# Later block loads and transposes, and a state copied on ScalarE, in a hybrid RWKV-7 and pooling layer

## Chip, cores, metric

One core of one Trainium2 chip runs the whole layer. The metric is the device time of one execution in microseconds (us); the median of several executions counts.

## What is computed

One layer on 1024 latent and 256 context tokens, model width 2048: RMS norm with modulation, one input projection whose columns feed an RWKV-7 time-mixing branch (16 heads of 64, two directions) and a pooling branch, gates on both, one output projection, a residual and a last norm. What the change touches is the scan of the time-mixing branch:

```python
def _rwkv_step(S, inp):
    r, w, k, v, a, b = inp
    sa = jnp.einsum('dbhvk,dbhk->dbhv', S, a)
    S = S * w[..., None, :] + sa[..., :, None] * b[..., None, :] + v[..., :, None] * k[..., None, :]
    y = jnp.einsum('dbhvk,dbhk->dbhv', S, r)
    return S, y
```

The state starts at zero, runs over the context tokens and then over the latent ones, forwards and backwards. The y of both directions are added, normalised per head, given a bonus, and multiplied by a gate.

## The kernel before

The scan is done in chunks of 64 tokens (20 chunks, 4 of them context). Four groups Q of four heads follow one another, so there are 80 steps: step k is one chunk of one Q, in both directions. Within a chunk the recurrence is a triangular system. Its matrices (the scores) are made by matmuls 20 steps ahead (`scores`, L758), copied by ScalarE and masked by GpSimd (`masked`, L771 and L772), and written to DRAM (sNM, L773). For 8 steps at a time VectorE inverts the diagonal 32x32 blocks of these matrices: `inverse` (L778) loads them as TT by four DMAs on SyncE's queue (L783), and then does 30 pairs of a multiply (L789) and an add (L791). `assemble` completes the inverses to 64x64 tiles T by two groups of small matmuls (L826, L837) through bank B0.

`run_step` (L1036) is one step:

- `phase_x` (L893): product of NA (scores and keys, from DRAM) and SUV. SUV holds, side by side on the partitions, the values from DRAM (`step_loads`, L856) and the state scaled to this step. VectorE copies the result to Xs (L896).
- the outputs of the step before (`outputs`, L935 and L937; L937 reads the state that was there before that step), then `step_loads`, `bk_load` and `score_loads` issue loads for later steps on SyncE.
- `phase_t` (L903): product with T; VectorE copies the result U into SUV (L904, L905).
- y is gathered (L957 on ScalarE, L959 on VectorE), and the scores of step k + 20 are made.
- `phase_s` (L915): the update of the state from BKt and SUV. VectorE adds the old state (St, L918) and multiplies by the decay PCt straight into the state's place in the next step's SUV, in two halves of 64 partitions (L922). GpSimd multiplies the same sum once more into the tile S (L923), which the next outputs and the next sum read.
- `turned` (L881, L882) transposes the keys of the next step on TensorE through bank B0 and ScalarE copies them to BKt; `masked` follows.
- `pump` fills TensorE with units of the gate, pooling and output columns of the input projection (dense units: twelve matmuls of 512 columns, L154 to L156, counted at UNIT = 2.65 us), 1.55 of them per step, or 2 where no scores are left to make.

What else VectorE does runs as threads, generators that `slot` and `invert` advance while a model of the time (`at`) has room: weight splits, gates, pooling, inversion, and `finish`, which normalises y (L972 to L985), loads bonus and gate (L992), transposes y through bank B0 (L1001), and combines them (L1008, L1010). In it `yield 0` ends the present slot, and `yield from later()` waits until one more dense unit has been issued, except where `rush` forces a thread through: when a new Q begins, `gathered` (L943) settles what is left of `finish`.

The order on TensorE, VectorE and ScalarE is the one in which the code issues (a manual schedule); that of SyncE and GpSimd is set by the framework's scheduler from readiness and code order. Each engine takes its queue in order. SyncE's DMAs share 8 semaphores in turn, so that a ninth waits for the first to land.

`begin(i)` (L1030) creates the inversion of batch i and issues its TT loads. In the step with k % 8 = 4 it runs at the end, after the scores' masks; the inversion's arithmetic starts in the step with k % 8 = 6, right behind Xs (`invert`, L1018).

Of the kernel before, what the change touches and what calls it, by code (L numbers as in the profile page):

```python
# [11 lines left out]
ALU = mybir.AluOpType  # L12
# [47 lines left out]
def hybrid_layer_kernel(ctx: ExitStack, tc: tile.TileContext, I, out, dbg=None):  # L60
    nc = tc.nc
    mm = nc.tensor.matmul
    V, S, G = nc.vector, nc.scalar, nc.gpsimd
# [9 lines left out]
    def nm(s):  # L73
        cnt[0] += 1
        return f"{s}_{cnt[0]}"

    def bank(tag, bufs=1):
        return psum.tile([128, 512], F32, tag=tag, bufs=bufs, name=nm("ps"))
# [108 lines left out]
    with ExitStack() as p0:  # L187
# [89 lines left out]
        for k in range(2):  # L277
            u = hc_pool.tile([128, NALL + 4], F32, tag="k", bufs=2, name=nm("ue"))
# [63 lines left out]
    for k in range(2):  # L342
        s, u = p1.tile([128, NALL], F32, tag="A", name=nm("s")), early[k]
# [213 lines left out]
    with ExitStack() as p2s:  # L557
# [7 lines left out]
        hss = [slice(64 * h, 64 * h + 64) for h in range(2)]  # L565
# [17 lines left out]
        def later():  # L583
            due = unit_no[0] + 1
            while unit_no[0] < due and not rush[0]:
                yield 0
# [255 lines left out]
        nas, suv, mrs, rts, bkts, ins = {}, {}, {}, {}, {}, {}  # L842
# [43 lines left out]
        def phase_x(k):  # L886
            NA, SUV = nas.pop(k), suv[k]
            if steps[k][1] + steps[k][2] == 0:
                st["S"] = st.pop("S0")
            XU = st["XU"] = bank("XU")  # L890
            for u in range(4):
                for h in range(2):
                    mm(XU[hss[h], 64 * u:64 * u + 64], NA[:, h, u // 2, u % 2, :], SUV[:, h, u // 2, u % 2, :],  # L893
                       start=True, stop=True)
            Xs = st["Xs"] = p2.tile([128, 4, C], F32, tag="Xs", name=nm("Xs"))
            V.tensor_copy(Xs.rearrange("q u v -> q (u v)"), XU[:, 0:256])  # L896
# [10 lines left out]
        def phase_s(k):  # L907
            Q, g, s = steps[k]
            c = CCH * g + s
            SUV, S0, DY = suv[k], st["S"], bank(("DY", "B1")[k % 2])  # L910
            if c < NCH - 1:
                BKt = bkts.pop(k)
                for u in range(4):
                    for h in range(2):
                        mm(DY[hss[h], 64 * u:64 * u + 64], BKt[:, u // 2, u % 2, h, :], SUV[:, h, u // 2, u % 2, :],  # L915
                           start=True, stop=True)
                tmp = p2.tile([128, 4, C], F32, tag="St", name=nm("St"))
                V.tensor_tensor(tmp.rearrange("q u v -> q (u v)"), DY[:, 0:256], S0.rearrange("q u v -> q (u v)"), ALU.add)  # L918
                Sn = p2.tile([128, 4, C], F32, tag="S", bufs=2, name=nm("S"))
                pc = PCt[:, Q, c].rearrange("q p d -> q (p d)").unsqueeze(2).broadcast_to([128, 4, C])  # L920
                for h in range(2):
                    V.tensor_tensor(suv[k + 1][hss[h], h].rearrange("q p d v -> q (p d) v"), tmp[hss[h]], pc[hss[h]], ALU.mult)  # L922
                G.tensor_tensor(Sn, tmp, pc, ALU.mult)  # L923
                st["S"] = Sn
            if g:
                st["late"] = k, S0, DY
            else:
                suv.pop(k)
# [37 lines left out]
        def finish(Q, m, y):  # L966
            runs = (C * (6 - 2 * m), C * (8 + 2 * m))
            js = slice(2 * Q, 2 * Q + 2)
            mean = p2.tile([128, 8], F32, tag="mean", bufs=2, name=nm("mean"))
            rs = p2.tile([128, 8], F32, tag="rs", bufs=2, name=nm("rs"))  # L970
            yf = y.rearrange("q p r c v -> q (p r c) v")
            V.tensor_reduce(mean, yf, mybir.AxisListType.X, ALU.add)  # L972
            V.tensor_scalar(mean, mean, 1.0 / C, None, op0=ALU.mult)
            yield 0.7
            V.tensor_tensor(yf, yf, mean.unsqueeze(2).broadcast_to([128, 8, C]), ALU.subtract)
            sq = p2.tile([128, 8, C], F32, tag="sqy", bufs=2, name=nm("sqy"))
            S.activation(sq, yf, AF.Square)
            yield 0.7
            yield from later()
            V.tensor_reduce(rs, sq, mybir.AxisListType.X, ALU.add)  # L980
            S.activation(rs, rs, AF.Sqrt, bias=eps_ln, scale=1.0 / C)
            yield 0.6
            yield from later()
            V.reciprocal(rs, rs)
            V.tensor_tensor(yf, yf, rs.unsqueeze(2).broadcast_to([128, 8, C]), ALU.mult)  # L985
            while gates_done[0] < 2 * Q + 2:
                unit()
            parts = []
            for src in (sBV, sG):
                t = p2.tile([128, 2, 2, 128], F32, tag="bvs", bufs=2 * BVS, name=nm("bvs"))  # L990
                for r in range(2):
                    dma(t[:, :, r], src[js, :, runs[r]:runs[r] + 128].rearrange("j q t -> q j t"))  # L992
                parts.append(t)
            yield 0.8
            yield 0
            while not dense[0] and not rush[0]:
                yield 0
            ps = bank("B0")
            for i in range(8):
                for h in range(2):  # L1000
                    mm(ps[hss[h], 64 * i:64 * i + 64], yf[hss[h], i, :], ident[hss[h], hss[h]], start=True, stop=True)  # L1001
            mx = p2.tile([128, 2, 2, 128], F32, tag="mxn", bufs=2, name=nm("mx"))
            for p in range(2):
                j = 2 * Q + p
                S.activation(mx[:, p].rearrange("q r t -> q (r t)"), ps[:, 256 * p:256 * p + 256], AF.Identity,
                             bias=lbs[:, j:j + 1], scale=lgs[:, j:j + 1])
            yield from later()
            V.tensor_tensor(mx, mx, parts[0], ALU.add)  # L1008
            yield 0.7
            V.tensor_tensor(mx, mx, parts[1], ALU.mult)  # L1010
            for r in range(2):
                idma(sM[js, :, runs[r]:runs[r] + 128].rearrange("j q t -> q j t"), mx[:, :, r])
            yield 0.7
# [16 lines left out]
        def begin(i):  # L1030
            if i < NST // 8:
                invs[i], invn[i] = inverse(i), 0
                next(invs[i])


        def run_step(k):  # L1036
            r = k % 8
            last = k == NST - 1
            phase_x(k)
            pe(0.7, st.get("suv", 0.0))  # L1040
            xs = dve(0.41, at["pe"])
            if r in (0, 5) and k // 4 + 1 < len(batches):
                asm["now"] = assemble(k // 4 + 1)
                next(asm["now"])
            late = st.pop("late", None)
            if late:
                outputs(*late)
                pe(1.7)
            else:
                unit()  # L1050
                owed[0] -= 1
            bk_load(k + 2)
            if not last:
                step_loads(k + 1)
            if k + LEAD + 2 < NST:
                score_loads(k + LEAD + 2)
            dense[0] = False
            invert(k, max(at["pe"], xs) + 0.5)
            slot(max(at["pe"], xs) + 0.4)
            phase_t(k)  # L1060
            pe(0.7, xs)
            us = dve(0.84, at["pe"])
            if late:
                gathered(*late)
                dve(0.56)
            if k + LEAD < NST:
                scores(k + LEAD)
                pe(1.7)
            elif unit_no[0] < NU:
                unit()  # L1070
                owed[0] -= 1
            if r in (2, 7) and "now" in asm:
                run(asm.pop("now"))
                pe(0.6)
            invert(k, max(at["pe"], us) + 0.5)
            slot(max(at["pe"], us) + 0.4)
            dense[0] = True
            phase_s(k)
            pe(0.7, us)
            st["suv"] = dve(1.48, at["pe"])  # L1080
            if not last:
                turned(k + 1)
                pe(0.6)
            if k + LEAD < NST:
                masked(k + LEAD)
            if r == 4:
                i = k // 8 + 1
                if i in invs:
                    run(invs.pop(i))
                begin(i + 1)  # L1090
            n = FILLS[k + LEAD >= NST]
            left = at["pe"] + UNIT * int(owed[0] + n) + 0.7
            slot(left - 1.2)
            invert(k, left)
            pump(n)
            if r in (1, 6) and "now" in asm:
                next(asm["now"])
                pe(0.6)
# [224 lines left out]
```

## Time and profile before

| what | us |
|---|---|
| median of 3 runs | 2368.15 |
| lowest and highest run | 2356.09, 2370.49 |
| the profiled execution | 2357.3 |
| its span, first to last instruction | 2355.5 |
| the scan's stretch in it | 1085 to 1955 |

The profile is of one execution. An engine's idle time counts only where it delays the end; a row's last part, in brackets or behind an arrow, is the idle time of the engine before that work and what ended it. PE is TensorE, DVE is VectorE, ACT is ScalarE, POOL is GpSimd, SPq is SyncE's queue of DMAs.

### The profile page before, as it was taken

How to read it: one execution, taken by the hardware profiler on the slowest of the kernel's cores; microseconds unless marked ns; L12 is line 12 of the kernel's file. 1: busy time of each engine (PE TensorE's matmuls, PEld its weight loads, DVE VectorE, ACT ScalarE, POOL GpSimd, SP SyncE). 2: the span in 40 equal slices, each digit the busy share in tenths (PEclk: the TensorE clock that was granted, in tenths of full speed). 3: DMA queues.
4: the chain of work that ended last, by engine and by line, in shares of the span. 5: the costliest groups of instructions: out<-in, count | busy, mean ns of one | idle time of the engine just before them, and what ended most of it. 6: DMA issues, size and time to landing. Idle time of an engine off the chain costs nothing. (4 is left out here: it accounts for less than half of the span.)

```text
span 2355.5 us, 49746 instructions
## 1 busy us (share of the span) xinstructions
PE 2155.2 (91%) x19854; PEld 1304.9 (55%) x19854; DVE 1474.1 (63%) x2544; ACT 849.3 (36%) x1447; POOL 514.0 (22%) x702
## 2 busy tenths in 40 slices
PE   2999999999999999989988989889799998999997
PEld 1445444454444444445655566556555664888886
DVE  7644756475476477456769767787586674445546
ACT  5344534344344344212223323323332223333424
POOL 3000000011000000244655555545443211000000
PEclk9999999999999999999999999999999999999999
DMA  8765555455343344796887788877877643645546
GB/s 307 232 211 171 141 146 149 140 150 154 100 127 96 104 127 112 221 299 193 249 238 226 212 237 243 258 220 231 232 232 198 187 136 104 219 130 170 192 129 206
DMA packets 494999, 437.19 MB, mean 186 GB/s; under 512 B 274328, under 2 KB 366520, under 8 KB 494512
## 3 DMA queue, kind: packets, MB, share of 16 engines
q1 hardware_dynamic: 473712, 366.88, 54.3%
q0 software_dynamic: 21056, 67.13, 8.4%
q8 instruction: 157, 2.57, 0.5%
q14 instruction: 74, 0.61, 0.1%
HBM read 316.68 MB, written 115.88 MB: 184 GB/s over the span
## 5 line engine op out<-in xcount | busy, mean ns | idle before, releaser
L154 PE MATMUL ps<-hhi,whi 128*128 128x512 f16 x1600 | 612.0, 383 | 1.6 <-DVE sg L686 0.8
L156 PE MATMUL ps<-hhi,wlo 128*128 128x512 f16 x1600 | 609.8, 381 | 0.6 <-DVE wlo L633 0.6
L155 PE MATMUL ps<-hlo,whi 128*128 128x512 f16 x1600 | 610.1, 382 | 0.0
L156 PEld LDWEIGHTS <-wlo 128*128 128x128 f16 x1888 | 185.5, 98 | 196.5 <-issue 17.5
L154 PEld LDWEIGHTS <-whi 128*128 128x128 f16 x1888 | 185.3, 98 | 192.4 <-issue 30.3
L155 PEld LDWEIGHTS <-whi 128*128 128x128 f16 x1888 | 185.8, 99 | 178.5 <-issue 21.8
L1181 PE MATMUL ps<-wolo,mhi 128*128 128x512 f32 x512 | 199.8, 390 | 2.7 <-DVE wolo L1177 2.6
L1181 PE MATMUL ps<-wohi,mlo 128*128 128x512 f32 x512 | 199.0, 389 | 0.0
L1181 PE MATMUL ps<-wohi,mhi 128*128 128x512 f32 x512 | 198.5, 390 | 0.0
L772 POOL TENSOR_TENSOR NM<-NM,mask 128x512 f32<-128x512 f32 (+1 forms) x140 | 177.8, 1288 | 54.9 <-ACT NM L771 51.0
L1177 DVE TENSOR_TENSOR wolo<-wo,wohi 128x512 fp32r<-128x512 f32 x144 | 98.2, 689 | 144.9 <-ACT wohi L1176 144.6
L147 DVE SCALAR_TENSOR_TENSOR wlo<-wraw,whi 128x512 f16<-128x512 f32 x104 | 70.6, 686 | 175.3 <-ACT whi L146 173.7
L1176 ACT CAST wohi<-wo 128x512 fp32r<-128x512 f32 x144 | 89.3, 621 | 174.6 <-PE ps L1181 156.3
L882 ACT COPY BKt<-ps 128x512 f32<-128x512 f32 x76 | 44.4, 584 | 283.3 <-PE ps L881 283.3
L896 DVE COPY Xs<-ps 128x256 f32<-128x256 f32 x80 | 33.8, 423 | 152.4 <-PE ps L893 152.1
L789 DVE TENSOR_TENSOR tm<-TT 128x30 f32<-128x30 f32 (+5 forms) x300 | 112.4, 375 | 14.0 <-DMA TT<-sNM 6.7
L923 POOL TENSOR_TENSOR S<-St,PCt 128x256 f32<-128x256 f32 x76 | 60.2, 792 | 264.4 <-DVE St L918 263.8
L791 DVE TENSOR_TENSOR TT<-TT,tm 128x30 f32<-128x30 f32 (+5 forms) x300 | 109.7, 366 | 10.3
L1181 PEld LDWEIGHTS ps<-wolo,mhi 128*128 128x128 f32 x512 | 96.1, 188 | 24.6 <-DVE wolo L1177 4.9
L1181 PEld LDWEIGHTS ps<-wohi,mhi 128*128 128x128 f32 x512 | 95.9, 188 | 21.0 <-ACT wohi L1176 1.0
L1181 PEld LDWEIGHTS ps<-wohi,mlo 128*128 128x128 f32 x512 | 96.1, 188 | 19.8
L758 PE MATMUL ps<-AR,BK 64*128 64x128 f32 (+1 forms) x1280 | 94.8, 289 | 8.2 <-issue 2.7
(232 smaller groups left out, 3523.7 us busy)
## 6 DMA issues: line engine op xcount, KB each, us to landing
wraw<-in_w_in SPq DMA_DIRECT2D x200, 256.0 KB, 3.8
BK<-sBK SPq DMA_DIRECT2D x156, 256.0 KB, 4.1
wo<-in_w_out SPq DMA_DIRECT2D x144, 256.0 KB, 2.9
sNM<-NM POOLq DMA_DIRECT2D x64, 512.0 KB, 5.4
wa<-in_w_ada SPq DMA_DIRECT2D x112, 256.0 KB, 3.3
wg<-in_w_ada SPq DMA_DIRECT2D x64, 256.0 KB, 3.0
AR<-sAR SPq DMA_DIRECT2D x64, 256.0 KB, 5.0
MR<-sNM SPq DMA_DIRECT2D x64, 256.0 KB, 3.3
```

The lines of the kernel that those rows point to most:

```text
L147: V.scalar_tensor_tensor(wlo, raw, WS, whi, op0=ALU.mult, op1=ALU.subtract)
L154: mm(ps[:, :n], w[0][:, k, :], hi[kt][:, o:o + n], start=(kt == 0), stop=False)
L155: mm(ps[:, :n], w[0][:, k, :], lo[kt][:, o:o + n], start=False, stop=False)
L156: mm(ps[:, :n], w[1][:, k, :], hi[kt][:, o:o + n], start=False, stop=(kt == KT - 1))
L758: mm(ps[h][:, 64 * ns * u:64 * ns * (u + 1)], BK[hs, u // 2, u % 2, :], AR[hs, :, u // 2, u % 2, :], start=True, stop=True)
L772: G.tensor_tensor(nv, nv, mv, ALU.mult)
L789: V.tensor_tensor(tm, TT[:, 0:s, s:s + 1].broadcast_to([128, s, n]), TT[:, s:s + 1, s + 1:32].broadcast_to([128, s, n]), ALU.mult)
L791: V.tensor_tensor(TT[:, 0:s, s + 1:32], TT[:, 0:s, s + 1:32], tm, ALU.add)
L923: G.tensor_tensor(Sn, tmp, pc, ALU.mult)
L1176: S.copy(whi, raw)
L1177: V.tensor_tensor(wlo, raw, whi.bitcast(F32), ALU.subtract)
L1181: mm(banks[q, t], mix[k][m][:, tk], w, start=(k == order[0] and n == 0), stop=(k == order[-1] and n == 2))
```

## The change

Three edits. The product on GpSimd (L923) is replaced by two copies on ScalarE, each of which takes one half of the scaled state out of the next step's SUV; they are issued in `phase_s`, ahead of `turned` and `masked`. In `finish` the transposes of y wait for one more dense unit. `begin` is called in the step with k % 8 = 5, between `phase_t` and `phase_s`, in place of the end of the step with k % 8 = 4; the batch is the same.

```diff
@@ phase_s
                 for h in range(2):
                     V.tensor_tensor(suv[k + 1][hss[h], h].rearrange("q p d v -> q (p d) v"), tmp[hss[h]], pc[hss[h]], ALU.mult)
-                G.tensor_tensor(Sn, tmp, pc, ALU.mult)
+                for h in range(2):
+                    S.copy(Sn[hss[h]].rearrange("q u v -> q (u v)"), suv[k + 1][hss[h], h].rearrange("q p d v -> q (p d v)"))
                 st["S"] = Sn
@@ finish
             yield 0.8
-            yield 0
+            yield from later()
             while not dense[0] and not rush[0]:
                 yield 0
@@ run_step
+            if r == 5:
+                begin(k // 8 + 2)
             if r in (2, 7) and "now" in asm:
                 run(asm.pop("now"))
                 pe(0.6)
...
                 i = k // 8 + 1
                 if i in invs:
                     run(invs.pop(i))
-                begin(i + 1)
```

SyncE's queue, where the loads of TT are issued in the batch begun around steps 52 and 53. Before (NA_17760 and SUV_17761 are the loads of step 54, TT_17681 the batch's blocks):

```order
L866 DMA MR_17608<-sNM 128x2x256
L783 DMA TT_17681<-sNM 32x32x32
L747 DMA BK_17611<-sBK 128x512
L748 DMA AR_17610<-sAR 128x512
L783 DMA TT_17681<-sNM 32x32x32 x3
L872 DMA BK_17758<-sBK 128x512
L851 DMA NA_17760<-sNM 64x256
L852 DMA NA_17760<-sAR 64x256
L856 DMA SUV_17761<-sV 64x2x64 x2
```

The same place in the changed kernel (SUV_17807 belongs to step 54, TT_17846 is the batch, AR_17820 holds the operands of the scores that follow those of step 53):

```order
L872 DMA BK_17804<-sBK 128x512
L856 DMA SUV_17807<-sV 64x2x64 x2
L783 DMA TT_17846<-sNM 32x32x32 x2
L864 DMA R_17816<-sAR 128x256
L866 DMA MR_17818<-sNM 128x2x256
L747 DMA BK_17821<-sBK 128x512
L748 DMA AR_17820<-sAR 128x512
L783 DMA TT_17846<-sNM 32x32x32 x2
```

The TT loads moved behind the NA and SUV loads of step 54, and half of them behind the next R, MR, BK and AR loads.

ScalarE around one `phase_s` and the work behind it, before (y is a gathered output, BKt the transposed keys, NM the scores, whi a dense weight):

```order
L957 COPY y_10737<-ps_10623 128x2x64 x2
L882 COPY BKt_10768<-ps_10769 128x512
L771 COPY NM_10775<-ps_10740 128x4x2x64
L771 COPY NM_10775<-ps_10741 128x4x2x64
L631 ACTIVATE whi_10813<-wraw_10670 128x512
```

And now (line numbers of the changed kernel; S_10773 is the state tile, SUV_10713 the next step's operand):

```order
L958 COPY y_10746<-ps_10631 128x2x64 x2
L924 COPY S_10773<-SUV_10713 64x256 x2
L882 COPY BKt_10778<-ps_10779 128x512
L771 COPY NM_10785<-ps_10749 128x4x2x64
L771 COPY NM_10785<-ps_10750 128x4x2x64
L631 ACTIVATE whi_10823<-wraw_10679 128x512
```

The two state copies stand ahead of the copies that empty bank B0 and the banks of the scores.

TensorE at the first transposes of y that have moved, before (L837 completes an assembly, L915 is phase_s, whi a dense weight):

```order
L837 MATMUL ps_12225<-T_11796,Rp_12120 32x32 x32
L915 MATMUL ps_12266<-SUV_11987,BKt_12050 64x64 x8
L1001 MATMUL ps_12303<-ident,y_10737 64x64 x16
L154 LDWEIGHTS whi_11306
L154 MATMUL ps_11944<-hhi_115,whi_11306 128x512
```

And now, one step further on (L881 transposes the next step's keys, L1002 is L1001 of before):

```order
L758 MATMUL ps_12427<-AR_12017,BK_12018 128x128
L881 MATMUL ps_12441<-ident,BK_12168 128x128 x4
L1002 MATMUL ps_12455<-ident,y_10746 64x64 x16
L154 LDWEIGHTS whi_11601
L154 MATMUL ps_12481<-hhi_107,whi_11601 128x512
```

These transposes moved from behind phase_s of one step to behind the next key transposes.

## Rows read from the trace of the kernel before

**Rows 1.** The page, busy time of TensorE, share of the span, instructions

```profile
PE 2155.2 (91%) x19854; PEld 1304.9 (55%) x19854; DVE 1474.1 (63%) x2544; ACT 849.3 (36%) x1447; POOL 514.0 (22%) x702
```

**Rows 2.** Busy time of each engine in the scan's stretch, with its columns

```profile
core 0: us, PE busy (x) PEld busy (x) DVE busy (x) ACT busy (x) POOL busy (x), PEclk, DMA share, GB/s
...
1085.00:1955.00 870.00, 780.16 (x11638) 515.31 (x11638) 629.57 (x1360) 264.21 (x513) 396.63 (x478) 0.97 0.75 216
```

**Rows 3.** TensorE's waits in the scan: us in total, times, longest

```profile
PE ps L915 <- DVE SUV L904: 19.3, 26, 3.0
PE ps L893 <- DMA SUV<-sV: 15.1, 8, 6.6
...
PE ps L1001 <- DVE y L985: 10.3, 3, 5.2
PE ps L1001 <- ACT BKt L882: 5.8, 8, 0.7
PE ps L903 <- DVE Xs L896: 5.6, 8, 1.0
PE ps L893 <- DVE SUV L922: 4.9, 10, 1.1
...
PE ps L826 <- ACT BKt L882: 1.5, 2, 0.7
```

**Rows 4.** Timeline of SyncE's queue in steps 4 and 52: start, length, line, what

```profile
1132.94 1.64 SPq L783 DMA_DIRECT2D TT<-sNM  x2
...
1669.59 0.32 SPq L783 DMA_DIRECT2D TT<-sNM  x1
...
1671.05 5.02 SPq L783 DMA_DIRECT2D TT<-sNM  x3
...
1678.30 0.90 SPq L851 DMA_DIRECT2D NA<-sNM  x1
...
1682.89 1.24 SPq L856 DMA_DIRECT2D SUV<-sV  x2
```

**Rows 5.** Timeline of TensorE, first product of step 54

```profile
1685.21 0.44 PE L893 MATMUL ps<-SUV,NA 128*64 128x64 f32 x2 [6.65 <-DMA SUV<-sV]
```

**Rows 6.** Timeline of VectorE, first inversion multiply in steps 6 and 54

```profile
1147.57 0.19 DVE L789 TENSOR_TENSOR tm<-TT 128x30 f32<-128x30 f32 x1
...
1687.42 0.19 DVE L789 TENSOR_TENSOR tm<-TT 128x30 f32<-128x30 f32 x1
```

**Rows 7.** DMA issues of TT: KB each, median us from issue to landing

```profile
TT<-sNM SPq DMA_DIRECT2D x40, 128.0 KB, 5.1
```

**Rows 8.** Timeline of TensorE, the three transposes of y that waited for VectorE

```profile
1288.52 1.98 PE L1001 MATMUL ps<-ident,y 64*64 64x64 f32 x32 [5.23 <-DVE y L985]
...
1361.36 1.98 PE L1001 MATMUL ps<-ident,y 64*64 64x64 f32 x32 [3.53 <-DVE y L985]
...
1708.51 1.72 PE L1001 MATMUL ps<-ident,y 64*64 64x64 f32 x32 [1.57 <-DVE y L985]
```

**Rows 9.** ScalarE's groups by form in the scan: busy us, mean ns, idle before

```profile
L957 ACT COPY y<-ps 128x128 f32<-128x128 f32 x64 | 13.9, 269 | 62.8 <-PE ps L937 62.8
...
L771 ACT COPY NM<-ps 128x256 f32<-128x256 f32 x24 | 7.9, 385 | 0.0
```

**Rows 10.** Timeline of one step's end, all engines

```profile
1390.14 0.66 PE L881 MATMUL ps<-ident,BK 128*128 128x128 f32 x4
1390.32 0.42 DVE L918 TENSOR_TENSOR St<-ps,S 128x256 f32<-128x256 f32 x1 [0.23 <-PE ps L915]
1390.77 1.18 DVE L922 TENSOR_TENSOR SUV<-St,PCt 64x256 f32<-64x256 f32 x2
1390.88 0.58 ACT L882 COPY BKt<-ps 128x512 f32<-128x512 f32 x1 [4.25 <-PE ps L881]
1390.88 0.78 POOL L923 TENSOR_TENSOR S<-St,PCt 128x256 f32<-128x256 f32 x1 [1.93 <-DVE St L918]
```

## Prediction

> **What bounds the kernel now.** I read the page's busy times first, then the scan's stretch in the windows view, then who waits for whom on TensorE there, and last single steps in the timeline. TensorE is busy 91% of the span [rows 1]. All three edits act in the scan alone (80 steps, 1085 to 1955 us). There TensorE is busy 780.16 of 870 us at a granted clock of 0.97 [rows 2], so 90 us are idle, and since the change removes no matmul, those 90 us are all that it can win and the place where it can lose. The reader is to see in [rows 3] how they split: waits for the U copies on VectorE (19.3 us, 26 times), for loads of SUV from DRAM (15.1, 8 times), for the normalised y (10.3, 3 times), for ScalarE to empty bank B0 (5.8 and 1.5, 10 times), for the state products (4.9, 10 times). Each is small; the order of instructions decides which ones stay.
>
> **Edit 1: the block loads (begin) half a step later.** They are four loads of TT, 10 batches in all, 8 of them in the steps that change. In the batch begun in step 52 the queue holds them from 1669.59 to 1676.07, before the loads of step 54, which start at 1678.30 and end at 1684.13 [rows 4]. TensorE then stands 6.65 us before the first product of step 54 [rows 5], waiting for SUV. In the new order the step's NA and SUV loads go first, two TT loads follow, and two more come behind the next R, MR, BK and AR loads. So the waits for SUV can go: 15.1 us [rows 3].
>
> What is late next is the inversion. Its first multiply stands right behind the Xs copy of step 54 (1687.42 [rows 6]) and ahead of the U copies on VectorE, which phase_s waits for. The TT loads move back by the 5.8 us that the step's loads take (1678.30 to 1684.13), so their issue ends near 1676.07 + 5.8 = 1681.9, and with the median 5.1 us to landing [rows 7] they are there at 1687.0. Without the wait of 6.65 the multiply would be ready at 1687.42 - 6.65 = 1680.8. It stalls 6.2 us; TensorE has outputs, phase_t and scores to do meanwhile and some 0.5 us beyond, so 5.7 us of the 6.65 come back as a wait for U. In a batch with no wait for SUV there is more room: in step 4's the issue ends at 1134.58, landing is near 1139.7, and the multiply comes at 1147.57 [rows 4, 6], 7.9 us later, more than the 5.8 us of the move. So I charge 5.7 for step 54 and half of the other 15.1 - 6.65 = 8.5 us of waits, 4.2: 9.9 given back. Bounds: nothing given back, or 5.7 in all eight batches, 45.6.
>
> **Edit 2: the transposes of y behind the next dense unit.** Of the three waits for the normalised y, 5.23 and 1.57 us belong to transposes that follow in the filling slot; the third, 3.53 [rows 8], stands behind phase_t, where a batch's unfinished work is forced through, and there later() lets it pass at once, so it stays. TensorE now does dense matmuls in that time, which it would have to do anyway. Gain 6.8 us; bounds 0 (VectorE is as late for the next Xs copy as it was for y) and 10.3.
>
> **Edit 3: ScalarE copies the state.** GpSimd's product of 128x256 goes, 76 of them; 152 copies of 64x256 come onto ScalarE. ScalarE is busy only 264 of 870 us [rows 2] and takes 385 ns for 128x256 out of PSUM [rows 9]. The trace has no copy of ScalarE's between two SBUF tiles, so it lies between the 0.27 of half the columns [rows 9] and the 0.58 of twice as many (L882 [rows 10]); I take the same columns' 0.385. That is 59 us of ScalarE, none of it on a path by itself. The new S is ready about 0.5 us after the second state product; it is read first by the outputs of the next step, which come after that step's whole first product.
>
> What counts is the queue. In a plain step [rows 10] L881 ends at 1390.80, ScalarE empties B0 (L882) at 1390.88, and the copies of the scores follow. Now L882 stands behind the state copies, which wait for the state products: St ends at 1390.74, the first product at 1391.19, the second at 1391.64, the copies end near 1391.68 and 1392.1, so L882 starts 1.27 us later. The bank has a second user directly behind L881 in 9 places of the new order (7 groups of transposes of y, where before there were 9, and 2 assemblies, as before); at each, TensorE waits 1.27 us more: 11.4 us. If VectorE itself comes late to St, by as much as its longest lateness for U, 3.0 us [rows 3], each grows by that: 9 x 4.27 = 38. With copies of 0.27 it is 9 x 1.04 = 9.4. Elsewhere a dense unit follows L881, which the code's own table puts at 2.65 us, and covers it. If that cover went, each step would lose 1.27.
>
> The gain of the edit is on VectorE. The two state products take 1.18 us together where two at 0.42, the time of the sum before them with the same columns, and the short gap would take 0.87: 0.31 us too long, while GpSimd's product runs [rows 10]. TensorE waits directly for these 10 times, 3.1 us. It waits 26 times for the U copies, later on the same queue; 0.31 each would be 8.1 more. I take the middle of 3.1 and 11.2: 7.1. The masks on GpSimd start 1.27 us later too and may then run beside the multiplies before the U copies; what those lose, VectorE's work before them wins, so I cost it at nothing, with 26 x 1.27 = 33 us as its far end.
>
> The Trainium skill (SBUF — State Buffer, section Who interferes with whom) says that an operation of VectorE with two SBUF inputs and a GpSimd operation that reads SBUF exclude each other for a whole instruction. The trace agrees in kind: the first product, already running, kept its length and the second, begun beside GpSimd's, was held; but for 0.31 us, not for the whole 0.78 of GpSimd's product. By the rule at its dearest the 76 products would hold VectorE for 76 x 0.78 = 59 us, by the row for 76 x 0.31 = 24.
>
> **Sum.** -15.1 + 9.9 - 6.8 + 11.4 - 7.1 = -7.7 us. The profiled execution took 2357.3 us (span 2355.5 and 1.8 around it), 10.9 below the median of the runs, 2368.15. So 2349.6 on its scale and 2360 on the median's.
>
> **Rivals.** *Inversion late in every batch* (slower): the TT landing takes over as the last thing in all eight batches, 5.7 us each, 45.6 for 9.9: -7.7 + 35.7 = +28, 2396. It decides as soon as the last TT load lands after the Xs copy of the next step, the one where the new inversion begins. For it: two of the four loads now stand behind AR, which waits for the scores of the same step. Against it: the 7.9 us of room in [rows 4, 6]. *The change doesn't do what it says* (the queue is bound by landings, and SUV comes late wherever TT stands): nothing of 15.1 comes, 9.9 of stalls does not either, or half of it: -7.7 + 15.1 = +7.4 at most, 2376. For it: the queue issued with hardly a pause around 1670 to 1690. Against: the waits sit just behind the TT loads. *GpSimd's hold on VectorE is the root of VectorE's lateness* (faster): the waits for U copies and state products, 19.3 + 4.9 = 24.2 us, and 5.6 for Xs, all go in place of 7.1: -7.7 - 22.7 = -30, 2338. For it: the hold in [rows 10]. Against: the masks, the larger GpSimd load, stay.
>
> **How the numbers follow.** Forecast 0.47, inversion late 0.18, loads late anyway 0.20, the hold as the root 0.15. A measurement of this kernel tells about 1% (23.7 us) from no change. Below 2344.5 lies nearly all of the third rival (0.13) and the lucky edge of the forecast (0.06); above 2391.8 half or more of the first (0.11) and 0.02 of the second. So faster 0.19, within 1% 0.68, slower 0.13. The forecast's own range is 2345 to 2378: from no stall for TT, copies of 0.27 and VectorE's larger gain, to 15 us of stalls, 20 at the copies and the smaller gain; to hold 8 in 10 it has to reach to most of both outer cases, 2338 to 2390.
>
> **What would show it.** Edit 1 right: TensorE's wait for SUV loads falls below 5 us; a new wait of VectorE's first inversion multiply for TT appears, some 10 us in total. Edit 2: the waits for y shrink to the one behind phase_t. Edit 3: the pair of state products takes 0.87 us everywhere, and the waits for L882 before L1001 and L826 grow from 7.3 to about 18 us. The prediction is wrong if TensorE's idle time in the scan falls by over 25 us, or grows; a wait of VectorE for TT over 30 us would be the first rival, and an unchanged wait for SUV the second.

## The result, and the profile after

In ten runs of each the changed kernel took 2378.93 us (median; 2367.90 to 2385.46) and the kernel before 2360.72 us (2353.93 to 2370.49): the ratio of the means is 1.0067, 95% interval 1.0050 to 1.0084. It is slower by 0.7%, some 16 us. That lies inside the bound of 1% that the prediction drew for no change, but ten runs of each do tell it from no change. The forecast was 2360, its own range 2345 to 2378. The profiled execution took 2377.1 us (span 2375.3), 19.8 more than the one of before.

The page after the change, its first rows and TensorE's granted clock:

```profile
span 2375.3 us, 49861 instructions
...
PE 2174.2 (92%) x19854; PEld 1312.8 (55%) x19854; DVE 1445.4 (61%) x2544; ACT 912.1 (38%) x1599; POOL 447.1 (19%) x626
...
PEclk9999999999999999999998899999999999999999
```

VectorE and GpSimd do less, ScalarE more, as meant. But TensorE is busy 19.0 us longer than in [rows 1], with the same 19854 matmuls. The scan's stretch, which is now 1085 to 1975, in the windows view:

```profile
core 0: us, PE busy (x) PEld busy (x) DVE busy (x) ACT busy (x) POOL busy (x), PEclk, DMA share, GB/s
...
1085.00:1975.00 890.00, 798.92 (x11629) 521.47 (x11629) 600.43 (x1359) 327.61 (x666) 329.31 (x401) 0.95 0.74 210
```

Against [rows 2]: idle time 890 - 798.92 = 91.1 us, where it was 89.8; busy time 798.92, where it was 780.16; granted clock 0.95, where it was 0.97. So of the 20 us that the stretch grew by, 1.2 are idle time and 18.8 are busy time. These windows are cut by hand; from the first L893 of the scan to the last, the growth is 19.9 us, 2.4 idle and 17.5 busy. Either way nearly all of it is TensorE taking longer for its work. Who waits for whom on TensorE, and VectorE's wait for TT, in the scan:

```profile
PE ps L915 <- DVE SUV L904: 42.4, 31, 4.7
...
PE ps L1002 <- ACT BKt L882: 11.0, 7, 2.4
PE ps L903 <- DVE Xs L896: 5.0, 3, 3.4
PE ps L826 <- ACT BKt L882: 4.3, 4, 1.9
...
PE ps L893 <- DVE SUV L922: 1.1, 1, 1.1
...
DVE tm L789 <- DMA TT<-sNM: 15.1, 5, 4.4
```

(L1002 is L1001 of before.) Held against [rows 3]: the waits for SUV loads (15.1) and for y (10.3) are gone from the list, those for the state products fell by 3.8 and those for Xs by 0.6; the waits for U grew by 23.1, and those for bank B0 from 5.8 + 1.5 to 11.0 + 4.3, by 8.0. The sum is +1.3, near what the idle time grew by. In total the waits were exchanged one for one. What changed is their length: in the scan TensorE has 8 pauses of 1.5 us or more before (27.2 us) and 19 after (45.4 us).

One place shows what the exchange cost. The timeline of TensorE in and behind step 36 (start, length, line, what, and in brackets the idle time before it):

```profile
1497.40 0.38 PE L154 MATMUL ps<-hhi,whi 128*128 128x512 f16 x1
...
1503.33 1.57 PE L915 MATMUL ps<-SUV,BKt 128*64 128x64 f32 x16 [1.87 <-DVE SUV L904]
...
1507.56 1.97 PE L1002 MATMUL ps<-ident,y 64*64 64x64 f32 x32 [1.61 <-ACT BKt L882]
1509.47 0.61 PE L154 MATMUL ps<-hhi,whi 128*128 128x512 f16 x1
1510.72 0.63 PE L154 MATMUL ps<-hhi,whi 128*128 128x512 f16 x1
...
1514.19 0.38 PE L154 MATMUL ps<-hhi,whi 128*128 128x512 f16 x1
```

and the windows view of the same stretch:

```profile
1494.00:1500.00 6.00, 5.87 (x90) 3.98 (x92) 5.01 (x14) 3.00 (x6) 1.74 (x2) 1.00 0.91 268
1500.00:1503.33 3.33, 1.46 (x30) 1.20 (x24) 3.13 (x9) 0.00 (x0) 2.53 (x4) 1.00 0.87 300
1503.60:1513.80 10.20, 8.46 (x63) 5.02 (x62) 7.07 (x13) 3.91 (x8) 5.44 (x8) 0.50 0.91 266
1513.80:1520.00 6.20, 6.20 (x95) 4.22 (x93) 2.38 (x7) 2.18 (x3) 3.36 (x5) 1.00 1.02 252
```

TensorE pauses 1.87 us for U, runs sixteen small matmuls and four transposes, and pauses 1.61 us for B0. Over 10.2 us it is granted 0.50 of its clock, 1.2 in place of 2.4 GHz, and a dense matmul takes 0.61 to 0.63 us where it takes 0.38 before and after. The two pauses are 3.5 us; the slow clock costs about half of the 8.46 busy us besides. The clock falls at 1503.60, 0.27 us behind the end of the wait for U and ahead of the wait for B0: the fall belongs to the first pause, and whether the second one drew it out is not shown here.

The trace's clock records, added up from the first L893 of the scan to the last, give 47.8 us at half clock in 9 stretches before the change and 95.6 us in 18 after it (the rounded clocks of the windows say about the same: 2 x 0.03 x 870 = 52, 2 x 0.05 x 890 = 89). At half clock half of the time is lost where TensorE is busy all through, so the added 47.8 us are worth up to 23.9 (TensorE was busy in 38.4 and in 85.5 us of them, which makes 23.6). That covers the 17.5 us of busy time; the scan, first L893 to last, grew from 859.3 to 879.2, by 19.9.

Laid beside TensorE's records, each stretch begins behind a pause, or while one is still open. Before: 4 behind pauses ahead of the first product L893, 3 behind a wait for y, 2 behind a wait for U. After: 10 behind waits for U (in two of these a wait for B0 follows), 3 behind waits for B0, 5 behind others. The longest pauses of before (6.65 for SUV, 5.23 and 3.53 for y) had been few; more, shorter ones took their place.

### The profile page after: what moved, and what is told of

The parts are those of the page before. It is cut to its first block, busy times and chain, and to the rows that moved or that the text cites. A ratio compares the mean times of both kernels' runs of the same rounds, so it can differ in the third digit from the quotient of the medians.

```text
span 2375.3 us, 49861 instructions
## 1 busy us (share of the span) xinstructions
PE 2174.2 (92%) x19854; PEld 1312.8 (55%) x19854; DVE 1445.4 (61%) x2544; ACT 912.1 (38%) x1599; POOL 447.1 (19%) x626
## 4 chain that ended last, share of the span: by engine, by line
PE 37%; DVE 9%; DMA 3%; issue 2%; ACT 1%; SPq 1%; DVEq 0%; POOL 0%; ACTq 0%; POOLq 0%
PE ps L1183 14%; PE ps L154 4%; PE ps L155 4%; PE ps L156 4%; DVE tm L789 2%; PE ps L893 2%; DMA TT<-sNM 2%; DVE TT L791 1%; PE ps L881 1%; PE ps L915 1%; PE ps L684 1%; PE ps L758 1%; PE ps L826 1%; PE ps L903 1%; PE ps L938 1%
## 5 line engine op out<-in xcount | busy, mean ns | idle before, releaser
L155 PEld LDWEIGHTS <-whi 128*128 128x128 f16 x1888 | 186.9, 99 | 181.7 <-issue 27.2
L772 POOL TENSOR_TENSOR NM<-NM,mask 128x512 f32<-128x512 f32 (+1 forms) x140 | 170.2, 1234 | 262.8 <-ACT NM L771 207.3
L924 ACT COPY S<-SUV 64x256 f32<-64x256 f32 x152 | 61.2, 403 | 325.8 <-DVE SUV L922 323.9
L1178 ACT CAST wohi<-wo 128x512 fp32r<-128x512 f32 x144 | 89.3, 621 | 177.3 <-PE ps L1183 157.9
L789 DVE TENSOR_TENSOR tm<-TT 128x30 f32<-128x30 f32 (+5 forms) x300 | 113.1, 377 | 30.7 <-DMA TT<-sNM 22.5
L791 DVE TENSOR_TENSOR TT<-TT,tm 128x30 f32<-128x30 f32 (+5 forms) x300 | 111.5, 372 | 10.3
L915 PE MATMUL ps<-SUV,BKt 128*64 128x64 f32 x1216 | 68.2, 237 | 46.6 <-DVE SUV L904 42.4
```

The costliest lines, as they stand in the source:

```text
L155: mm(ps[:, :n], w[0][:, k, :], lo[kt][:, o:o + n], start=False, stop=False)
L772: G.tensor_tensor(nv, nv, mv, ALU.mult)
L789: V.tensor_tensor(tm, TT[:, 0:s, s:s + 1].broadcast_to([128, s, n]), TT[:, s:s + 1, s + 1:32].broadcast_to([128, s, n]), ALU.mult)
L791: V.tensor_tensor(TT[:, 0:s, s + 1:32], TT[:, 0:s, s + 1:32], tm, ALU.add)
L1178: S.copy(whi, raw)
```

## The experiments

The theory after this look: the change trades few long pauses for more short ones, at nearly no loss of idle time, and the loss is the clock that the added pauses take from TensorE. The rivals: the waits themselves are the loss (TT late in SyncE's queue; the state copies ahead of L882 in ScalarE's), or one of the three edits is the whole of it.

All ratios are of means, to runs of the kernel before in the same session. "Half clock" is the time at 0.5 in the scan of the profiled execution, with the number of stretches; idle is TensorE's in the scan, first L893 to last. The last column is worked out from the granted clock on record for every run: twice the lost share, times the span, averaged; it is of the whole execution, and in brackets stands the same for the kernel before in that session (for the changed kernel's there is none; the row of before has the range of the four others).

| kernel | median us | ratio (95%) | scan us | half clock us | idle us | half clock, all runs us |
|---|---|---|---|---|---|---|
| before | | 1 | 859.3 | 47.8 (9) | 88.7 | 82.1 to 87.3 |
| after | 2378.93 | 1.0067 (1.0050 to 1.0084) | 879.2 | 95.6 (18) | 91.1 | 117.4 |
| begin_alone | 2364.02 | 1.0041 (1.0021 to 1.0060) | 865.1 | 61.4 (14) | 89.3 | 89.0 (82.1) |
| later_alone | 2354.29 | 0.9990 (0.9968 to 1.0012) | 853.7 | 44.4 (11) | 85.1 | 82.3 (82.1) |
| copy_alone | 2369.25 | 1.0061 (1.0038 to 1.0085) | 874.4 | 78.5 (16) | 92.6 | 102.1 (82.1) |
| copy_behind | 2357.89 | 1.0012 (0.9994 to 1.0031) | 857.6 | 58.0 (10) | 87.6 | 93.1 (82.1) |
| fill_both | 2366.28 | 1.0040 (1.0021 to 1.0059) | 868.8 | 27.3 (6) | 73.4 | 67.4 (87.3) |
| fill_else | 2389.07 | 1.0136 (1.0110 to 1.0162) | 892.4 | 88.7 (17) | 88.9 | 118.6 (87.3) |
| inv_late | 2369.59 | 1.0047 (1.0026 to 1.0068) | 870.7 | 78.5 (16) | 90.1 | 111.6 (87.3) |
| begin_early | 2370.83 | 1.0050 (1.0029 to 1.0071) | 875.7 | 85.3 (17) | 91.8 | 113.3 (87.3) |
| no_begin | 2350.26 | 0.9967 (0.9947 to 0.9986) | 850.9 | 58.0 (10) | 79.0 | 81.0 (83.7) |
| behind_inv | 2349.95 | 0.9969 (0.9946 to 0.9992) | 854.6 | 54.6 (11) | 82.4 | 93.6 (83.7) |
| early_inv | 2343.08 | 0.9929 (0.9903 to 0.9955) | 844.6 | 51.2 (13) | 72.4 | 80.2 (83.7) |
| early_inv_pool | 2354.60 | 0.9982 (0.9957 to 1.0007) | 856.7 | 51.2 (11) | 84.2 | 88.2 (84.9) |

The times before, by session: 2354.91 (begin_alone to copy_behind), 2358.94 (fill_both to begin_early), 2358.14 (no_begin to early_inv) and 2360.64 (early_inv_pool).

The last column guards against reading too much from one execution: the kernel before by itself goes from 51 to 104 us of half clock between its runs, so two single traces that differ by 20 us say little. Over its 102 runs in the four sessions, a straight line through time against half clock rises by 0.49 us per us (correlation 0.75): the half that was put on it above is what those runs show. By the column the change added 30 to 35 us of half clock, worth 15 to 18 us, and the kernel lost 16. By this estimate the clock is nearly the whole loss.

### Which edit costs: one at a time

Each is the kernel before with one hunk of the change:

```diff
 begin_alone                      later_alone               copy_alone
-begin(i + 1)   # r == 4, end    -yield 0                  -G.tensor_tensor(Sn, tmp, pc, ALU.mult)
+begin(k // 8 + 2)  # r == 5     +yield from later()       +S.copy(Sn[half], suv[k + 1][half])  # x2
```

> Only the later call of begin. Theory A (many short waits make TensorE run at half clock): the loads of SUV no longer stop TensorE (15.1 us become under 4), the first inversion multiply waits for TT in about 5 to 7 batches, the waits for the U copies grow by 15 to 25 us, and the half-clock time in the scan grows by 15 to 30 us; 8 to 15 us slower than before. Theory B (only the waits count, the clock is chance): 3 to 8 us slower, half-clock time within 10 us of before.

> Only the later transposes of y. A: two waits of 5.2 and 1.6 us go, and the 6.8 and 3.4 us at half clock right behind them too; 7 to 12 us faster than before. B: 5 to 7 us faster, half-clock time as before.

> Only the copies on ScalarE, in place of the product on GpSimd. A: the waits for bank B0 (L882 before L1001 and L826) go from 7.3 to 17 to 20 us in pieces of about 2 us, the waits for state products fall by 3, and the half-clock time grows by 10 to 20 us; 5 to 15 us slower than before. B: 5 to 10 us slower with half-clock time as before. That GpSimd's product held VectorE (third rival of the prediction) would make it faster.

TensorE's waits for U and VectorE's for TT in begin_alone:

```profile
PE ps L915 <- DVE SUV L904: 34.5, 29, 6.6
...
DVE tm L789 <- DMA TT<-sNM: 7.8, 4, 3.0
```

and TensorE's in copy_alone:

```profile
PE ps L915 <- DVE SUV L904: 26.7, 29, 2.4
PE ps L1002 <- ACT BKt L882: 15.3, 9, 2.8
PE ps L893 <- DMA SUV<-sV: 6.5, 3, 5.1
...
PE ps L826 <- ACT BKt L882: 5.0, 4, 2.6
```

Two edits cost time by themselves, the loads (+0.41%) and the copies (+0.61%); the transposes do nothing that can be measured, where 5 to 12 us had been expected of them: the waits for y leave the list, those for Xs grow from 5.6 to 8.7 us. With the loads later, the 15.1 us of waits for SUV go and 15.2 come back at U (19.3 to 34.5), of which the waits for TT explain about half. With the copies ahead of L882, the B0 waits go from 7.3 to 20.3 us: 13.0, for an estimate of 11.4. Added, the three make 1.0092; together they measured 1.0067. In the two edits that cost, the idle time moved by 0.6 and 3.9 us in the traces, and the half-clock time by 13.6 and 30.7; over all runs the half-clock time moved by 6.9 and 20.0. So the clock is worth some 10 of the 14 us that the copies cost, but only 3.5 of the 10 that the loads cost: what the rest of the loads' cost is stays open.

### ScalarE's queue

The changed kernel with the two copies issued behind the copies of the scores:

```diff
@@ phase_s
-                for h in range(2):
-                    S.copy(Sn[hss[h]]..., suv[k + 1][hss[h], h]...)
+                st["copy"] = Sn, suv[k + 1]
@@ run_step
                 masked(k + LEAD)
+            if "copy" in st:
+                Sn, SUV = st.pop("copy")
+                for h in range(2):
+                    S.copy(Sn[hss[h]]..., SUV[hss[h], h]...)
```

> The changed kernel, but the two state copies are issued behind the copies that empty bank B0 and the score banks. A and B: the waits for B0 go back to about 7 us, so 8 to 11 us less waiting than in the changed kernel; A adds 3 to 8 us of half-clock time saved: 11 to 17 us faster than the changed kernel, about 2364 to 2368. B: 8 to 11 us, 2368 to 2371. If the next outputs or sum wait for the later S, L937 or St shows it and the gain is smaller.

TensorE's waits in it:

```profile
PE ps L915 <- DVE SUV L904: 42.5, 29, 7.9
...
PE ps L1001 <- ACT BKt L882: 5.0, 7, 0.7
...
PE ps L826 <- ACT BKt L882: 1.5, 2, 0.7
...
DVE tm L789 <- DMA TT<-sNM: 15.8, 5, 7.6
```

The B0 waits are back at 6.5 us, and the waits for U are as long in total as in the changed kernel (42.5). In the traces idle time fell by 3.5 us, half-clock time by 37.6, and the scan by 21.6; this execution was the fastest of its twelve, so that overstates it. By the ratios, of 1.0067, 1.0012 is left, which no measurement here tells from 1: 13 us less. Over all runs the half-clock time fell by 24, worth 12. So the position of the copies in ScalarE's queue, ahead of L882, accounts for most of the loss, and most of it came through the clock.

### The clock by itself

If the pauses' price is the clock, useless matmuls in them must make the kernel faster. fill_both is the changed kernel with 152 matmuls of 512 columns more, whose results nobody reads: 10 ahead of phase_s in the 8 steps where an inversion begins, and 8 behind L881 in the 9 places where another user of B0 follows directly. At the spacing of the dense matmuls, 0.216 us, they are 32.8 us of work. fill_else is the control: 10 in each step with k % 8 = 3, where no inversion begins. It was meant to add 80; it ran in 9 steps and added 90, 19.4 us:

```profile
L1083 PE MATMUL ps<-hhi 128*128 128x512 f16 x90 | 22.2, 396 | 0.0
```

```diff
+            if r == 6 and k // 8 + 2 in invs:          # fill_else: r == 3 and k // 8 + 1 in invs
+                ps = bank("B0")
+                for _ in range(10):
+                    mm(ps, hhi[0][:, 0:128], hhi[0][:, 0:512], start=True, stop=True)
             dense[0] = True
             phase_s(k)
...
+            filler()                                   # fill_both alone: 8 of the same into bank XU
             ps = bank("B0")
             for i in range(8):
```

> The changed kernel with 152 matmuls whose result nobody reads, 32.8 us of TensorE's work at 0.216 us each: 10 before phase_s in each of the eight steps where an inversion begins, 8 before each use of bank B0 that stands right behind L881 (9 places). The order is otherwise the same. Theory A (the waits' price is the half clock behind them): half-clock time in the scan falls from 96 to under 65 us, and the time falls by 5 to 14 us although there is more to do. Theory B (the waits alone): 3 to 10 us slower than the changed kernel, as the filling is longer than some waits.

> Control: the changed kernel with 80 such matmuls, 10 before phase_s in the steps with k % 8 = 3, where no new wait stands. A and B: 8 to 17 us slower than the changed kernel, half-clock time within 10 us of its 96.

The same place as above in fill_both (step 36, without an inversion's beginning; L971 are the eight added matmuls, L1009 is L1002):

```profile
1495.70 1.14 PE L915 MATMUL ps<-SUV,BKt 128*64 128x64 f32 x16 [1.88 <-DVE SUV L904]
1496.77 0.65 PE L881 MATMUL ps<-ident,BK 128*128 128x128 f32 x4
1497.26 1.89 PE L971 MATMUL ps<-hhi 128*128 128x512 f16 x8
1499.93 1.15 PE L1009 MATMUL ps<-ident,y 64*64 64x64 f32 x32 [0.78 <-ACT BKt L882]
```

and in the windows view, the whole scan's stretch and what follows the place:

```profile
1085.00:1975.00 890.00, 816.61 (x11807) 525.43 (x11807) 609.71 (x1376) 332.80 (x672) 331.89 (x403) 0.98 0.73 212
1497.00:1503.00 6.00, 5.22 (x54) 2.88 (x53) 3.80 (x8) 3.91 (x8) 2.88 (x4) 1.00 0.91 275
1503.00:1513.00 10.00, 10.00 (x127) 6.53 (x126) 7.15 (x14) 3.71 (x7) 6.32 (x9) 1.00 1.08 248
```

The pause for U is the same, 1.88 us. The second pause is filled but for 0.78, the clock stays at 1.00, and the 32 transposes take 1.15 us where they took 1.97. Why the clock did not fall behind the pause for U here, as it did in the changed kernel ahead of any filling, is not shown, so the reading rests on the scan as a whole and not on this place. Over the scan half-clock time falls from 95.6 to 27.3 us in the traces, and from 117.4 to 67.4 over all runs, worth 25 us.

The kernel with 32.8 us more work is not slower: 1.0040 against 1.0067, 0.27% or 6.4 us less, though the two intervals overlap. Of the 32.8 us, 17.7 went into pauses (idle time 91.1 to 73.4), so a theory in which pauses cost their length alone has to expect some 15 us more; with 25 us given back by the clock the expectation is 10 less. The measurement is on the side of the clock. The control tells what such matmuls cost elsewhere: 1.0136 - 1.0067 = 0.69%, 16.3 us for 19.4 of work, with the half-clock time of all runs where it was (118.6).

### Where the inversion waits for its loads

inv_late is the changed kernel without the first of a step's two calls of the inversion where a batch begins, so that its first multiply stands behind the U copies. begin_early issues the TT loads right behind step_loads, ahead of phase_t and of the scores.

```diff
 inv_late                                          begin_early
-invert(k, max(at["pe"], xs) + 0.5)               step_loads(k + 1)
+if r != 6:                                       +if r == 5:
+    invert(k, max(at["pe"], xs) + 0.5)           +    begin(k // 8 + 2)
```

> The changed kernel, but in the step where an inversion begins its first multiplies come behind the U copies and not before them. A and B: VectorE's wait for TT falls from 15 to under 5 us, the waits for the U copies from 42 to 20 to 27. A: half-clock time down by 20 to 30 us as well, 12 to 20 us faster than the changed kernel (ratio to before 0.998 to 1.002). B: only 5 to 10 us faster, as other waits take the place.

> The changed kernel, but begin is called at the start of the step with k % 8 = 5, right behind its step_loads, so that TT is not queued behind the score loads of that step. If the second half of TT behind AR is what made it late: VectorE's wait for TT falls from 15 to under 5 us, no wait for SUV comes back, 10 to 16 us faster than the changed kernel. If TT is late because the queue itself is full: wait for TT of 8 to 15 us remains, and at most 6 us faster.

TensorE's waits in inv_late:

```profile
PE ps L915 <- DVE SUV L904: 22.9, 25, 2.1
PE ps L826 <- ACT BKt L882: 15.4, 7, 5.5
PE ps L1002 <- ACT BKt L882: 11.6, 6, 2.5
```

Out of U's way, the wait for TT did not go: 10.9 us of 15.1 are left, where under 5 had been expected. VectorE, stopped at its first multiply, comes late to what stands behind it; the longer waits for L882 fit state products that come late and hold ScalarE's copies and L882 behind them, a reading of the order that no run tests by itself. The waits for U fell by 19.5 us and those for B0 rose by 11.7. The gain, 0.20%, is within the intervals; 12 to 20 us had been expected. In begin_early VectorE still waits 14.1 us for TT and TensorE 42.0 for U: so it was not their place behind AR that made two of the four loads late. That the queue is full of the step's loads there is the reading that is left, not one that a run shows; the 0.17% between its ratio and the changed kernel's is within the intervals.

### Together

no_begin leaves the loads where they were and has the transposes and the copies behind; behind_inv is copy_behind with the inversion's late start; early_inv is behind_inv with the loads right behind step_loads; early_inv_pool is early_inv with GpSimd's product in place of the copies.

```diff
 early_inv against the kernel before               early_inv_pool against early_inv
+if r == 5: begin(k // 8 + 2) # at step_loads      -st["copy"] = Sn, suv[k + 1]
+yield from later()                                +G.tensor_tensor(Sn, tmp, pc, ALU.mult)
+st["copy"] = ... # copies behind masked
+if r != 6: invert(...)   # the first of two
```

> The kernel before with two of the three edits: the later transposes of y, and the state copies on ScalarE, issued behind the copies that empty bank B0 and the score banks; begin stays where it was. If the copies cost only by their place in ScalarE's queue, and GpSimd's product did hold VectorE: waits for B0 near 7 us, waits for SUV about 15 us, waits for the U copies 15 to 20, half-clock time in the scan 40 to 50 us; 3 to 12 us faster than before (ratio 0.995 to 0.999). If the product's hold was worth nothing, 0.999 to 1.001; if the later S is itself late, above 1.001.

> The changed kernel with both mends: copies behind, first inversion multiplies behind the U copies. If the two new waits are all that made it slower: waits for U below 25 us, for B0 near 7, for SUV below 4, half-clock time below 50 us; 2 to 10 us faster than before (ratio 0.996 to 0.999). If the load queue is simply full, TT is still waited for by 10 us and the ratio is 1.000 to 1.003.

> As the run before, with begin right behind step_loads in the step with k % 8 = 5. If TT then lands in time: VectorE's wait for TT below 5 us and 2 to 5 us faster than the run before. If its landing is set by the full queue: no difference of over 3 us.

> As early_inv, but with GpSimd's product kept in place of the copies on ScalarE: what the third edit is worth by itself where its place in the queue costs nothing. If the product's hold on VectorE (0.31 us in the second state product) reaches TensorE in part: 2344 to 2356, that is 2 to 10 us slower than early_inv. If it is hidden anyway: the same as early_inv within 2 us.

TensorE's and VectorE's waits in early_inv:

```profile
PE ps L915 <- DVE SUV L904: 15.1, 21, 1.7
...
PE ps L893 <- DMA SUV<-sV: 10.4, 10, 1.9
...
PE ps L1001 <- ACT BKt L882: 4.3, 6, 0.7
...
PE ps L826 <- ACT BKt L882: 1.5, 2, 0.7
...
DVE tm L789 <- DMA TT<-sNM: 6.2, 3, 3.4
```

The first two gain 0.33% and 0.31%. In behind_inv the waits for U fall to 14.7 us, but the waits for SUV loads are back at 15.0 (14 times, the longest 3.1), where under 4 had been expected, and VectorE's for TT are 18.4. Here SUV comes late although TT stands behind it, as in the prediction's second rival; the changed kernel itself had no such wait. early_inv gains 0.71% (0.9903 to 0.9955) and beats both kernels: its idle time is 72.4 us, 16 less than before, and its longest waits for U and SUV are 1.7 and 1.9 us. Its half-clock time over all runs is 80.2 us, against 83.7 before: this gain is idle time, not clock. Without the copies (early_inv_pool) 0.18% is left, within the noise: the two ratios differ by 0.53%, some 12 us, and their intervals just do not meet, so the third edit, once its copies stand behind L882, is worth more than the other parts. The idle time differs by the same 12 us, 72.4 and 84.2.

## Why the prediction was wrong, step by step

**The step that failed** is in its first part: "since the change removes no matmul, those 90 us are all that it can win and the place where it can lose". The busy time was taken as given. It is given only at a given clock, and of the 20 us lost in the scan 17.5 to 18.8 are busy time. [Rows 2] had the sign of it, a granted clock of 0.97, which means 3% of the stretch was lost already, and the waits in [rows 3] had to be priced a second time by what the clock does behind them.

The Trainium skill (TensorE: Matmul & The Clock Gate, section HAM oscillation) tells of a kernel whose waits between bursts let the clock fall, and adds half of the throttled time to the cost. The trace here agrees: half of the 47.8 us added is 23.9, and the scan grew by 19.9.

**The base** was off too. The forecast stood on the median of three runs, 2368.15; ten runs gave 2360.72. As a change, -7.7 us was forecast and some +16 measured. That 2360 came within 0.8% of the time measured is in part luck: by the ten runs it would have been 2353.

**The sum of the waits** came out at +1.3 in place of -7.7, 9.0 us off. By its terms:

- Waits for SUV -15.1: right, they left the list.
- Given back at U, +9.9 less 4.0 of the 7.1 won on VectorE: the waits for U should have ended at 25.2 and ended at 42.4. This term was mis-sized by 17.2, and it splits by step. In the steps with k % 8 = 6, where an inversion begins, the waits for U went from 1.1 to 18.3 us, +17.2 where 9.9 was charged: VectorE waited 15.1 us for TT, not some 10. In all other steps they went from 18.2 to 24.1, +5.9 where -4.0 was forecast. The copies ahead of L882 do that: in copy_alone these steps have 24.9, in copy_behind 16.2. The first rival, late in every batch, was half true: five waits of eight batches, the longest 4.4.
- The masks beside the inversion's multiplies were costed "at nothing". The timeline of all engines in one step of the changed kernel:

```profile
1397.23 2.50 POOL L772 TENSOR_TENSOR NM<-NM,mask 128x512 f32<-128x512 f32 x2
...
1397.67 2.27 DVE L789 TENSOR_TENSOR tm<-TT 128x168 f32<-128x168 f32 x1
...
1402.04 1.14 PE L915 MATMUL ps<-SUV,BKt 128*64 128x64 f32 x16 [2.12 <-DVE SUV L904]
```

  A multiply of 168 columns takes 2.27 us beside the masks, where the 19 others of that size in this kernel take 0.32 to 0.34, and TensorE waits 2.12 us for U behind it. Before, the same multiply took 1.50 beside a mask, with a wait of 1.36. All multiplies together take 112.4 us before and 113.1 after, so what the masks take is about the same and it falls elsewhere: in the scan TensorE waits for U behind 4 of the multiplies longer than 0.7 us before (4.6 us in all), and behind 8 after (9.6 us). These 5 us are most of the 5.9 of the other steps.
- Transposes of y, -6.8 forecast: -10.3; the wait that was to stay behind phase_t went too. later_alone shows that this bought nothing measurable.
- B0 waits, from 7.3 to about 18: 15.3. Right in mechanism and near in size. What the sum missed is what the clock adds: with the copies behind, the kernel is 13 us faster, 3.5 us of it idle time in the traces.
- State products: the pair takes 0.87 us as forecast. The groups by line, changed kernel:

```profile
L922 DVE TENSOR_TENSOR SUV<-St,PCt 64x256 f32<-64x256 f32 x152 | 63.8, 420 | 5.1 <-DMA SUV<-sV 0.2
L924 ACT COPY S<-SUV 64x256 f32<-64x256 f32 x152 | 61.2, 403 | 325.8 <-DVE SUV L922 323.9
```

  and before:

```profile
L922 DVE TENSOR_TENSOR SUV<-St,PCt 64x256 f32<-64x256 f32 x152 | 85.9, 565 | 4.9
```

  One product fell from 565 to 420 ns, so 152 of them by 22.1 us, near the 24 by the prediction's row. The copies took 403 ns for 385 assumed.

**The rival on GpSimd's hold** was priced at -30. In the change as made it did not decide; with the copies behind L882 and the inversion out of the way the edit was worth some 12 us (early_inv against early_inv_pool).

**What would show it** named both outcomes: idle time that "falls by over 25 us, or grows" would prove the forecast wrong. It grew, by 1.2 to 2.4 us, hardly at all; the mark itself looked in the wrong column, at idle time and not at busy time.

## What to carry to other kernels

Before pricing a change to a kernel that TensorE bounds, read the granted clock beside the busy time, and price a pause of TensorE twice: its length, and the matmuls that may run at half clock behind it. Here the added half clock cost some 15 us or more, the added idle time 1 to 2, and useless matmuls in the pauses gave back 25 us of clock for the 15 us of them that the pauses did not hold. One trace is one execution: compare the granted clock of all runs before calling it a cause. Work that waits for another engine belongs behind the copies that empty a bank in the same queue, not ahead of them.

## What the runs showed that was not expected

- With the idle time equal within 2.4 us, two orders of the same matmuls differ by 17.5 us of TensorE's busy time in the scan, which the granted clock covers (half-clock time 47.8 and 95.6 us).
- 32.8 us of added matmuls in 17 chosen places cost nothing and seem to gain 6.4 us; 19.4 us of the same matmuls in 9 other places cost 16.3.
- ScalarE's copy between two SBUF tiles, 64x256, takes 403 ns, more than the 385 of twice the partitions out of PSUM.
- Not every pause lowers the clock: in fill_both 1.88 us for U, at the place shown, left it at 1.00, while in the changed kernel half clock followed 1.87 us at the same place. What decides between such pauses was not settled.
- The kernel before, run again and again, goes from 51 to 104 us of half clock by the granted clock of its runs (0.989 to 0.978): its time, 2336 to 2372 us, rises by about half of what the half clock rises by.
